# Context tokens of a feed-forward product: seven units in plain FP32 ahead, nine inside the seven-product steps, with the modulation and the second product's loads re-placed

## The chip, the cores and the metric

One Trainium2 chip; the kernel runs on 1 of its cores, as one launch. The metric is the device time of that launch in microseconds (us). Engines are called PE (matrix multiply), DVE (vector), ACT (scalar), POOL (GpSimd) and SP (the queue from which most DMAs are issued); each takes its own instructions in order and waits for others through semaphores. SBUF is the on-chip memory with 128 partitions, PSUM the eight accumulator banks that PE writes.

## The reference, cut to what matters

Two layers of one trunk run over 256 context tokens (two tiles of 128) and 1024 latent tokens (eight tiles). All is float32. Each layer ends in a feed-forward part for both streams; the second layer needs no context output.

```python
def _ffn_sublayer(x, shift, scale, gate, p):
    h = _modulate(_rms_norm(x, p['g_pre_ffn']), shift, scale)
    f = jnp.square(jax.nn.relu(h @ p['w_ff1'])) @ p['w_ff2']
    return x + gate * _rms_norm(f, p['g_post_ffn'])

    mod = s_lat @ w_mod[i] + b_mod[i]        # six shift/scale/gate vectors, latent stream
    mod_c = s_ctx @ w_mod[i] + b_mod[i]      # the same for the context stream
```

`w_ff1` is 1024 x 4096, `w_ff2` 4096 x 1024, `w_mod` 1024 x 6144 for each layer. Ahead of the feed-forward part each layer has a mixer (attention, short convolution, a state-space scan); the change leaves it alone.

## The kernel before, in words

**Split products.** A float32 operand is kept as two tiles in the reduced format fp32r: a high part (ACT, a cast) and a low part (source minus high part, DVE or POOL). `mm3` (lines 90 to 92) makes a product of three matmuls: high x high, high x low, low x high.

**First product, latent tokens.** For one of 16 units `j` of `w_ff1` the eight latent tiles are multiplied by Strassen's scheme in Winograd's form: seven products of halves in place of eight. `parts` makes the seven token operands `s0`..`s6` (512 tokens wide, from the four pairs of tiles that `all_pairs` normalises and transposes), `w1_parts` makes the seven weight operands of a unit from two raw loads `fraw`. `step1` runs the products on PE, seven times four times `mm3` = 84 matmuls of 512 columns, combines them with DVE (`u`, `c`), ACT (ReLU, then square) and POOL (`q`), and `combine` writes seven combinations to DRAM (`a7`) through ACT's DMA queue. PE's order in this whole part is the order in which the program is written; the other engines' instructions are placed by the scheduler of the language.

**First product, context tokens.** In the first layer this runs ahead of the 16 steps. `context` loops over all 16 units: `cut` splits each quarter of the weights (`craw` into `cwh`, `cwl`), `mm3` multiplies with the context tokens `hch`, `hcl`, 48 matmuls of 256 columns a unit; ReLU and square follow on ACT into two tiles `cab` with one buffer each, the combinations on POOL, seven small DMAs on ACT's queue. Between its blocks `side` weaves in `all_pairs`.

**Modulation of the next layer.** `mod_half` makes a quarter of one of the six vectors: four loads `mraw` of 256 KB through a ring of two buffers, and for each of 8 row blocks and each stream one DVE instruction (first L80, then L160) on an accumulator `acc`; at the end PE sums over partitions (L166, or L192 for gates). There are 24 such tasks, 8 of them for two streams. A list `bg` feeds them through `tick`: ten in steps 1 to 10, the others in the second product.

**Second product.** `second` goes over granules of the reduced dimension (one pair of units, then three times two pairs), with seven products each (`ORDER2`), five token pairs in the first layer, four in the second: 1470 and 1176 matmuls of 512 columns. It reads `a7` back (`ar`, ring of two) and the raw `w_ff2` (`graw`, in `w2`, four quarters of a unit at the start of a granule), splits both (`w2h`, `w2l`, `a2h`, `a2l`) and accumulates in SBUF. The last pair of units goes through `plain`.

Of the kernel before, what the change touches and what calls it, by code (L numbers as in the profile page):

```python
# [6 lines left out]
F32 = mybir.dt.float32  # L7
# [33 lines left out]
def emit(tc, A, depth=DEPTH):  # L41
# [127 lines left out]
    def mod_half(mp, L, v, half, streams, mb, nk, nb, off=False):  # L169
        accs = {s: mp.tile([P, mb], F32, tag="acc", name="acc", bufs=2 * 512 // mb) for s in streams}  # L170
# [16 lines left out]
        for s in streams:  # L187
# [5 lines left out]
            rows, rowb = (mp.tile([P, nk, mb], F32, tag="raw", name=n_, bufs=nb)[:, 0, :] for n_ in ("mrow", "mrowb"))  # L193
# [124 lines left out]
    class Strassen:  # L318

        def __init__(self, L, pairs, ctx=None):
# [7 lines left out]
        def load(self, p_, t, nb):  # L330
            xt = self.x[t] = p_.tile([P, D], F32, tag="x", name="x", bufs=nb)
            dma(xt, x1_d[t])
            normed(fp, xt, xt)
# [37 lines left out]
        def parts(self, p, what, alt="v"):  # L371
# [9 lines left out]
            for w in what:  # L381
                if w == "e":
# [6 lines left out]
                    put(5, s2, alt)  # L389
                    yield  # L390
                elif w == "a":
# [4 lines left out]
                    put(1, a12, "p")  # L396
# [3 lines left out]
                elif w == "b":  # L400
                    put(6, a21, alt)
                    yield
                else:
# [3 lines left out]
                    put(3, a22, "p")  # L407
# [9 lines left out]
        def w1_parts(self, j, out):  # L417
# [16 lines left out]
            tt("v", b22, b22, t1, ALU.subtract)  # L434
            t2 = b22
            put(5, t2, "v")
            put(4, t1, "v")
            put(1, b21, "p")
            put(6, t3, "v")
            yield  # L440
# [3 lines left out]
        def step1(self, j, w):  # L444
            st, n = self.st, self.n

            def t_(nm):
                return st.tile([P, n], F32, tag=nm, name=nm, bufs=1)
# [7 lines left out]

            A_, B_, C_ = psum("s"), psum("s"), psum("s")
            p1, p5, u2, q, c12, c21, c22, r11 = (t_(nm) for nm in ("p1", "p5", "u2", "q", "c12", "c21", "c22", "r11"))
# [8 lines left out]
            self.relu2(r11, A_[:, :n])  # L467
            prod(B_, 6, False, True)
            tt("v", c22, B_[:, :n], q, ALU.add)
            prod(C_, 2, False, True)  # L470
            tt("v", c12, C_[:, :n], u2, ALU.add)
            prod(B_, 3, False, True)
            tt("v", c21, B_[:, :n], p1, ALU.add)
            self.relu2(c22, c22)
            self.relu2(c12, c12)
            self.relu2(c21, c21)
            self.combine(j, (0, n), r11, c12, c21, c22, q, u2, p5)
# [5 lines left out]
        def combine(self, j, cs, r11, c12, c21, c22, q, u2, p5, e="v"):  # L483
# [7 lines left out]
            tt(e, q, c21, c22, ALU.add)  # L491
            tt(e, u2, q, r11, ALU.subtract)
            tt(e, c21, r11, c21, ALU.subtract)
            tt(e, p5, c12, u2, ALU.subtract)
# [3 lines left out]
        def context(self, side):  # L498

            hh, hl_ = self.hc  # L500
            halves = [(j, q) for j in range(16) for q in range(2)]
            ready = []

            def fetch():
                if halves:
                    j, q = halves.pop(0)
                    r = (wr if j % 2 == 0 else self.rw).tile([P, WU // 2], F32, tag="raw", name="craw", bufs=2)
                    dma(r, A["wu"][self.L, U_FF1 + j, :, q * 1024:(q + 1) * 1024])
                    raws.extend([r[:, 0:512], r[:, 512:1024]])

            def cut():
                if not raws:
                    fetch()
                if raws:
                    w = [self.cw.tile([P, 512], F32R, tag="cw" + x_, name="cw" + x_, bufs=6) for x_ in "hl"]
                    split(*w, raws.pop(0), "a", "v")
                    ready.append(w)

            raws = []
            for _ in range(5):  # L520
                cut()
            for j in range(16):
                ps = psum("s"), psum("s")
                for kh in range(2):
                    for c in range(2):
                        w = ready.pop(0)
                        for k in range(4):
                            o = slice(k * P, (k + 1) * P)
                            mm3(ps[c][:, :256], (w[0][:, o], w[1][:, o]), (hh[:, 4 * kh + k, :], hl_[:, 4 * kh + k, :]),
                                kh == 0 and k == 0, kh == 1 and k == 3)  # L530
                        cut()
                        side(j)
                ca, cb = (self.co.tile([P, 256], F32, tag=f"c{i}", name="cab", bufs=1) for i in range(2))
# [3 lines left out]
                self.combine(j, (self.n, self.n2), ca[:, :P], cb[:, :P], ca[:, P:], cb[:, P:], q, u2, p5, "p")  # L537
# [16 lines left out]
        def w2(self, gs):  # L554

            r = {}
            for q in (0, 2, 3, 1):
                for g in gs:
                    p_, nb = (wr, 2) if q == 0 else (self.rw, 6)
                    x = r[q, g] = p_.tile([P, WU // 2], F32, tag="raw", name="graw", bufs=nb)  # L560
# [1302 lines left out]
```

## Time and profile before

| | us |
|---|---|
| median of 3 runs | 3105.79 (3103.48 to 3110.14) |
| the profiled execution's own time | 3108.29 |
| its span, first to last instruction | 3106.5 |
| first layer, context part, 816.0 to 975.0 | 159.0 |
| first layer, 16 steps, 975.0 to 1304.5 | 329.5 |
| first layer, second product up to `plain`, 1304.5 to 1692.5 | 388.0 |
| first layer, `plain`, 1692.5 to 1764.0 | 71.5 |
| second layer, second product up to `plain`, 2767.5 to 3052.0 | 284.5 |

Over the span PE is busy 91%, DVE 72%, ACT 46%, POOL 41%; PE's mean granted clock is 0.944 of full speed. A row of a group reads: line, engine, operation, output <- inputs, shapes, count | busy time, mean ns of one | idle time of the engine just before, and what ended it. The mean is the duration of one instruction, and matmuls overlap, so their pace is read from the distance of two starts in the timeline, not from the mean. A float32 matmul of unsplit operands appears as two records.

### The profile page before, as it was taken

How to read it: one execution, taken by the hardware profiler on the slowest of the kernel's cores; microseconds unless marked ns; L12 is line 12 of the kernel's file. 1: busy time of each engine (PE TensorE's matmuls, PEld its weight loads, DVE VectorE, ACT ScalarE, POOL GpSimd, SP SyncE). 2: the span in 40 equal slices, each digit the busy share in tenths (PEclk: the TensorE clock that was granted, in tenths of full speed). 3: DMA queues.
4: the chain of work that ended last, by engine and by line, in shares of the span. 5: the costliest groups of instructions: out<-in, count | busy, mean ns of one | idle time of the engine just before them, and what ended most of it. 6: DMA issues, size and time to landing. Idle time of an engine off the chain costs nothing.

```text
span 3106.5 us, 41599 instructions
## 1 busy us (share of the span) xinstructions
PE 2818.2 (91%) x14606; PEld 2353.0 (76%) x14606; DVE 2237.0 (72%) x3323; ACT 1416.0 (46%) x2701; POOL 1284.3 (41%) x1151
## 2 busy tenths in 40 slices
PE   7988979999878999898997989999888699989998
PEld 5877878867766788787775778788766488868887
DVE  6688748776676896487897767348776866646888
ACT  3443447734454545452232454247634555545332
POOL 4465726676364222232225444326655422223233
PEclk9988999989988999999998899999889799999999
DMA  6245551253455554455543433441243244454443
GB/s 230 83 136 176 179 145 26 63 158 121 152 181 161 180 192 162 163 196 181 181 155 98 157 105 115 150 148 24 86 133 114 92 153 152 150 182 151 155 136 125
DMA packets 256849, 438.48 MB, mean 141 GB/s; under 512 B 23392, under 2 KB 132720, under 8 KB 256640
## 3 DMA queue, kind: packets, MB, share of 16 engines
q1 hardware_dynamic: 197536, 348.35, 34.9%
q10 hardware_dynamic: 52704, 75.92, 6.8%
q0 software_dynamic: 6400, 11.56, 1.5%
q8 instruction: 115, 1.88, 0.2%
q14 instruction: 94, 0.77, 0.1%
HBM read 310.79 MB, written 124.95 MB: 140 GB/s over the span
## 4 chain that ended last, share of the span: by engine, by line
PE 59%; DVE 17%; DMA 8%; issue 7%; POOL 5%; ACT 3%; SPq 0%; ACTq 0%; POOLq 0%; DVEq 0%
PE ps_s L90 16%; PE ps_s L91 15%; PE ps_s L92 15%; DMA mraw<-w_mod 3%; DVE acc L160 2%; PE ps_t L1235 2%; DVE yo L76 2%; PE ps_o L90 2%; PE ps_o L92 2%; PE ps_o L91 1%; DVE acc L76 1%; DVE w2l L76 1%; PE ps_g L1255 1%; PE ps_g L1256 1%; DVE graw L76 1%
## 5 line engine op out<-in xcount | busy, mean ns | idle before, releaser
L90 PE MATMUL ps_s<-w2h,a2h 128*128 128x512 f32 x1026 | 409.6, 400 | 35.3 <-DVE yo L76 13.6
L91 PE MATMUL ps_s<-w2l,a2h 128*128 128x512 f32 x1026 | 407.0, 397 | 0.5 <-DVE w2l L76 0.5
L92 PE MATMUL ps_s<-w2h,a2l 128*128 128x512 f32 x1026 | 405.4, 395 | 2.2 <-DVE a2l L76 2.2
L76 POOL TENSOR_TENSOR a2l<-ar,a2h 128x1280 fp32r<-128x1280 f32 (+1 forms) x56 | 165.5, 2956 | 404.4 <-ACT a2h L71 399.0
L71 ACT CAST a2h<-ar 128x1024 fp32r<-128x1024 f32 (+1 forms) x105 | 121.4, 1156 | 395.5 <-PE ps_s L91 238.5
L90 PEld LDWEIGHTS ps_s<-w2h,a2h 128*128 128x128 f32 x1026 | 196.9, 192 | 84.9 <-ACT a2h L71 11.9
L71 ACT CAST wh<-fraw 128x512 fp32r<-128x512 f32 x224 | 138.1, 621 | 235.2 <-PE ps_s L91 112.0
L76 POOL TENSOR_TENSOR wl<-fraw,wh 128x512 fp32r<-128x512 f32 x64 | 94.0, 1470 | 349.8 <-ACT wh L71 304.3
L160 DVE SCALAR_TENSOR_TENSOR acc<-mraw,svec,acc 128x256 f32<-128x256 f32 (+1 forms) x280 | 213.8, 777 | 34.0 <-DMA mraw<-w_mod 31.7
L92 PEld LDWEIGHTS ps_s<-w2h,a2l 128*128 128x128 f32 x1026 | 196.2, 191 | 45.4 <-DVE a2l L76 3.3
L91 PEld LDWEIGHTS ps_s<-w2l,a2h 128*128 128x128 f32 x1026 | 196.5, 192 | 41.0 <-DVE w2l L76 1.0
L76 DVE TENSOR_TENSOR w2l<-graw,w2h 128x1024 fp32r<-128x1024 f32 x102 | 165.5, 1624 | 23.9 <-ACT w2h L71 21.1
L1207 DVE TENSOR_REDUCE sm<-ps_s 128x1 f32<-128x512 f32 (+1 forms) x200 | 117.5, 592 | 35.0 <-PE ps_s L92 31.5
L76 DVE TENSOR_TENSOR wl<-fraw,wh 128x512 fp32r<-128x512 f32 x160 | 110.5, 692 | 29.6 <-ACT wh L71 27.4
L1220 ACT ACTIVATE P<-ps_s,sm 128x512 f32<-128x512 f32 (+1 forms) x200 | 120.0, 612 | 13.6 <-DVE sm L80 10.7
L76 DVE TENSOR_TENSOR fraw<-fraw 128x512 f32<-128x512 f32 x128 | 106.8, 836 | 23.6 <-POOL wl L76 19.3
L76 DVE TENSOR_TENSOR pl<-ps_t,ph 128x512 fp32r<-128x512 f32 x164 | 110.0, 684 | 12.6 <-ACT ph L71 11.8
L71 ACT CAST ph<-ps_t 128x512 fp32r<-128x512 f32 x164 | 94.8, 588 | 50.5 <-PE ps_t L1235 45.4
L71 ACT CAST w2h<-graw 128x1024 fp32r<-128x1024 f32 x106 | 110.6, 1044 | 6.9 <-PE ps_s L92 4.9
L76 DVE TENSOR_TENSOR yo<-ps_s,yo 128x512 f32<-128x512 f32 x144 | 94.7, 680 | 19.3 <-PE ps_s L92 19.3
L90 PE MATMUL ps_s<-hch,cwh 128*128 128x256 f32 x256 | 80.3, 313 | 29.0 <-ACT cab L480 27.7
L277 POOL TENSOR_TENSOR ss<-ss,expn 128x1 f32<-128x1 f32 x74 | 48.7, 658 | 134.0 <-DVE ss L276 130.4
(519 smaller groups left out, 9043.3 us busy)
## 6 DMA issues: line engine op xcount, KB each, us to landing
ar<-a SPq DMA_DIRECT2D x52, 640.0 KB
fraw<-wu SPq DMA_DIRECT2D x64, 512.0 KB
graw<-wu SPq DMA_DIRECT2D x64, 512.0 KB
ar<-a SPq DMA_DIRECT2D x53, 512.0 KB
wraw<-wu SPq DMA_DIRECT2D x48, 512.0 KB
mraw<-w_mod SPq DMA_DIRECT2D x96, 256.0 KB
a<-c ACTq DMA_DIRECT2D x92, 256.0 KB
x<-x SPq DMA_DIRECT2D x40, 512.0 KB
```

What stands on the lines that cost most here:

```text
L71: nc.scalar.copy(out=out, in_=in_)
L76: (nc.vector if e == "v" else nc.gpsimd).tensor_tensor(out=out, in0=a, in1=b, op=op)
L90: nc.tensor.matmul(out, lhsT=sh, rhs=mh, start=first, stop=False, skip_group_check=more)
L91: nc.tensor.matmul(out, lhsT=sh, rhs=ml, start=False, stop=False, skip_group_check=more)
L92: return nc.tensor.matmul(out, lhsT=sl, rhs=mh, start=False, stop=last, skip_group_check=more)
L160: nc.vector.scalar_tensor_tensor(out=acc, in0=raw, scalar=svec[:, k, s:s + 1], in1=acc, op0=ALU.mult, op1=ALU.add)
L277: nc.gpsimd.tensor_tensor(out=out, in0=out, in1=expn[:, :n], op=ALU.pow)
L1207: nc.vector.tensor_reduce(out=self.sm[i][:, b:b + 1], in_=self.sp_[i, b][:, :self.blocks[b][1]], axis=AX.X, op=ALU.max)
L1220: nc.scalar.activation(out=self.Pt[i][:, b0:b0 + bn], in_=self.sp_[i, b][:, :bn], func=AF.Exp, scale=SCALE, bias=self.sm[i][:, 5:6], accum ...
L1235: nc.tensor.transpose(ps[:, (2 * kk + i) * P:(2 * kk + i + 1) * P], self.Pt[i][:, kt * P:(kt + 1) * P], ident)
L1255: nc.tensor.matmul(self.av[:, :256], lhsT=vt_, rhs=ph[:, kk, :], start=kt == 0, stop=False)
L1256: nc.tensor.matmul(self.av[:, :256], lhsT=vt_, rhs=pl[:, kk, :], start=False, stop=kt == self.nkt - 1)
```

## The change

**Units 0 to 6 of the context part** (`ALONE = 7`) stay ahead of the steps and are multiplied unsplit: one float32 matmul of raw weights `craw` and unsplit tokens `hc32` in place of each `mm3`. `cut` and its splits go. The combinations move from POOL to DVE. `side` takes three items a call, in 28 calls in place of 64; all low parts of the pairs' operands go to DVE, half of the transposes' evictions and the normalising multiplication to ACT, and four token tiles are loaded at once.

**Units 7 to 15** go into the steps: `merged(j)`. Three of the four weight quarters that the context tokens need are operands of the step already (0, 1, 2); the fourth, `b12`, is split as an eighth (7). `cprod` adds 4 x 12 matmuls of 256 columns between the step's products, into one further PSUM bank; the context columns then ride with the latent ones through square, `combine` (640 columns in place of 512) and one DMA.

**In all steps of both layers** the order of products is 0, 4, 5, 1, 6, 2, 3 (before 0, 5, 4, 1, 6, 2, 3), and the weights are split in that order. The weights' slots are 6 in the first layer (before 9) and 8 in the second (before 11).

**All 24 modulation tasks** run in the steps: one at each step's end, and from step 7 on (and in step 4) a second one in its middle. The single-stream tasks come first; from step 7 on a step has one of one stream and one of two. A task's PE part now comes two tasks later.

**Second product.** The quarters of `w_ff2` are loaded by `quarter`, between the `ar` loads and in the order in which the products use them, and the queue keeps that order. The buffers for `ar` come first in their region. In the first granule all low parts are made by DVE. The gate load `G` keeps its place in the program's order too.

PE, first layer, the start of the context part (`x` token tiles, `cst` the identity for transposes). Before:

```order
L294 MATMUL ps_g<-cst,x 128x128 x2
L294 MATMUL ps_t<-cst,x 128x128 x2
L90 MATMUL ps_s<-hch,cwh 128x256
L91 MATMUL ps_s<-hcl,cwh 128x256
L92 MATMUL ps_s<-hch,cwl 128x256
```

Now:

```order
L1522 MATMUL ps_t<-cst,x 128x128 x4
L558 MATMUL ps_s<-hc_8327,craw 128x256 x16
L364 MATMUL ps_t<-cst,x 128x128 x2
L364 MATMUL ps_g<-cst,x 128x128 x2
L364 MATMUL ps_t<-cst,x 128x128 x2
L558 MATMUL ps_s<-hc_8327,craw 128x256 x4
```

One row stands where three stood, and the latent pairs' transposes (L364) come after the first unit's 16 matmuls.

PE, first layer, step 7, from the first product to the next. Before:

```order
L90 MATMUL ps_s<-s0h,wh 128x512
L91 MATMUL ps_s<-s0l,wh 128x512
L92 MATMUL ps_s<-s0h,wl 128x512
L90 MATMUL ps_s<-s5h,wh 128x512
L91 MATMUL ps_s<-s5l,wh 128x512
L92 MATMUL ps_s<-s5h,wl 128x512
```

Now:

```order
L90 MATMUL ps_s<-s0h,wh 128x512
L91 MATMUL ps_s<-s0l,wh 128x512
L92 MATMUL ps_s<-s0h,wl 128x512
L90 MATMUL ps_t<-hch,wh 128x256
L91 MATMUL ps_t<-hcl,wh 128x256
L92 MATMUL ps_t<-hch,wl 128x256
```

Behind a product of the latent tokens come the context tokens' matmuls with the same weights, into the bank `ps_t`.

SP, first layer, the loads of the second product (`a_0_i_g` is combination `i` of pair of units `g`). Before:

```order
L104 DMA graw<-wu 128x1024 x2
L104 DMA G<-g_0_1_88 128x1024
L104 DMA ar<-a_0_0_0_6748 128x2x640
L104 DMA ar<-a_0_1_0_6756 128x2x640
L104 DMA ar<-a_0_2_0_6764 128x2x640
L104 DMA graw<-wu 128x1024 x3
L104 DMA ar<-a_0_4_0_6780 128x2x640
```

Now:

```order
L104 DMA ar<-a_0_0_0_6748 128x2x640
L104 DMA graw<-wu 128x1024
L104 DMA ar<-a_0_1_0_6756 128x2x640
L104 DMA graw<-wu 128x1024
L104 DMA ar<-a_0_2_0_6764 128x2x640
L104 DMA graw<-wu 128x1024
L104 DMA ar<-a_0_4_0_6780 128x2x640
```

`G` no longer stands ahead of the first `ar`, and each quarter of the weights stands behind the `ar` of its own product.

```diff
     def mod_half(mp, L, v, half, streams, mb, nk, nb, off=False):
-        accs = {s: mp.tile([P, mb], F32, tag="acc", name="acc", bufs=2 * 512 // mb) for s in streams}
+        accs = {s: mp.tile([P, mb], F32, tag="acc", name="acc", bufs=6 if mb < 512 else 2) for s in streams}
...
         def w1_parts(self, j, out):
...
             put(0, b11, "v")
             tt("v", b11, b12, b11, ALU.subtract)
-            t1 = b11
-            put(2, b22, "p")
+            t1 = t2 = b11
+            put(4, t1, "v")
             yield
+            tt("v", t2, b22, t1, ALU.subtract)
+            put(5, t2, "v")
+            put(1, b21, "p")
+            if self.merged(j):
+                put(7, b12, "p")
             tt("v", b12, b22, b12, ALU.subtract)
             t3 = b12
...
             put(6, t3, "v")
+            put(2, b22, "p")
             yield
...
+        def merged(self, j):
+            return self.ctx is not None and j >= self.ALONE
+
-        def step1(self, j, w):
+        def step1(self, j, w, mid):
...
+            def cprod(i, c, kh):
+                if mg:
+                    hh, hl_ = self.hc
+                    for k in range(4):
+                        o = slice(k * P, (k + 1) * P)
+                        mm3(X_[:, c * 256:c * 256 + 256], (w[i][0][:, o], w[i][1][:, o]), (hh[:, 4 * kh + k, :], hl_[:, 4 * kh + k, :]),
+                            kh == 0 and k == 0, kh == 1 and k == 3, True)
...
             prod(A_, 0, True, True)
-            copy("a", p1, A_[:, :n])
+            copy("a", p1[:, :n], A_[:, :n])
+            cprod(0, 0, 0)
+            prod(C_, 4, True, True)
+            copy("a", p5[:, :n], C_[:, :n])
+            tt("p", q[:, :n], p1[:, :n], p5[:, :n], ALU.add)
             prod(B_, 5, True, True)
-            tt("v", u2, B_[:, :n], p1, ALU.add)
-            prod(C_, 4, True, True)
-            copy("a", p5, C_[:, :n])
-            tt("p", q, p1, p5, ALU.add)
+            tt("v", u2[:, :n], B_[:, :n], p1[:, :n], ALU.add)
             prod(A_, 1, False, True)
...
         def context(self, side):
...
-            for j in range(16):
+            for j in range(self.ALONE):
                 ps = psum("s"), psum("s")
                 for kh in range(2):
+                    r = raws.pop(0)
                     for c in range(2):
-                        w = ready.pop(0)
                         for k in range(4):
-                            o = slice(k * P, (k + 1) * P)
-                            mm3(ps[c][:, :256], (w[0][:, o], w[1][:, o]), (hh[:, 4 * kh + k, :], hl_[:, 4 * kh + k, :]),
-                                kh == 0 and k == 0, kh == 1 and k == 3)
-                        cut()
+                            o = slice(c * 512 + k * P, c * 512 + (k + 1) * P)
+                            nc.tensor.matmul(ps[c][:, :256], lhsT=r[:, o], rhs=self.hc32[:, 4 * kh + k, :], start=kh == 0 and k == 0,
+                                             stop=kh == 1 and k == 3)
                         side(j)
+                    fetch()
...
+                    if first and i in (0, 1, 2, 4):
+                        self.quarter(r, {0: 0, 1: 2, 2: 3, 4: 1}[i])
+                    elif i == 1:
+                        self.quarter(r, 1)
+                    for q in {5: (2,), 3: (0, 3)}.get(i, ()):
+                        self.quarter(r + 1, q)
...
-            for v in (1, 0, 2, 4, 3, 5):
-                for half in range(4):
-                    ss_ = (1, 0) if v < 2 or L + 1 < depth - 1 else (0,)
-                    bg.append(lambda v=v, half=half, ss_=ss_: mod_half(box["mp"], L + 1, v, half, ss_, 256, 2, 2))
+            tasks = [[(v, h) for v in vs for h in range(4)] for vs in ((2, 4, 3, 5), (1, 0))]
+            while tasks[0]:
+                if len(tasks[0]) <= 8 and tasks[1]:
+                    bg.append(lambda v=tasks[1][0][0], h=tasks[1].pop(0)[1]: mod_half(box["mp"], L + 1, v, h, (1, 0), 256, 2, 2))
+                bg.append(lambda v=tasks[0][0][0], h=tasks[0].pop(0)[1]: mod_half(box["mp"], L + 1, v, h, (0,), 256, 2, 2))
...
-            fs.step1(j, w)
-            if not last and 0 < j < 11:
-                tick(defer=True)
+            fs.step1(j, w, lambda: tick(defer=2) if j == 4 or j > 6 else None)
+            tick(defer=2)
             w = nxt
...
+        fs.ar = le.enter_context(pool("ar"))
+        la3 = le.enter_context(pool("a3"))
         lac = le.enter_context(pool("ac"))
         acc = {i: [lac.tile([P, 512], F32, name=f"acc{i}_{p}") for p in range(np_)] for i in (0, 5, 6)}
-        la3 = le.enter_context(pool("a3"))
-        fs.ar = le.enter_context(pool("ar"))
         fs.rw = le.enter_context(pool("rw2"))
-        if not last:
-            box["mp"] = le.enter_context(pool("mp2"))
```

More of the change, by code (lines that the diff above doesn't have):

```diff
@@ L192, in mod_half @@
             nc.tensor.matmul(ps[0:32, :mb], lhsT=ones[:, 0:32], rhs=accs[s], start=True, stop=True)
-            rows, rowb = (mp.tile([P, nk, mb], F32, tag="raw", name=n_, bufs=nb)[:, 0, :] for n_ in ("mrow", "mrowb"))
+            rows, rowb = (mp.tile([P, mb], F32, tag="row", name=n_, bufs=2) if mb < 512 else
+                          mp.tile([P, nk, mb], F32, tag="raw", name=n_, bufs=nb)[:, 0, :] for n_ in ("mrow", "mrowb"))
             b0, p0 = R_BG1 + w * D + h0, R_GPOST + w * D + h0
@@ L369, in part2, with parts @@
                 pass
-        def parts(self, p, what, alt="v"):
+        def parts(self, p, what, alt="p"):
             h = self.h32[p]
@@ L472, in step1 @@
+            cprod(2, 1, 1)
+            side(c22, 3)
+            side(c12, 2)
             prod(B_, 3, False, True)
[L473 to L477, printed above, removed]
+            tt("v", c21[:, :n], B_[:, :n], p1[:, :n], ALU.add)
+            end(c22)
+            end(c12)
+            end(c21)
+            r11, c12, c21, c22, q, u2, p5 = (x[:, :m] for x in (r11, c12, c21, c22, q, u2, p5))
@@ L498, in context @@
         def context(self, side):
-            hh, hl_ = self.hc
-            halves = [(j, q) for j in range(16) for q in range(2)]
-            ready = []
+            halves = [(j, q) for j in range(self.ALONE) for q in range(2)]
+            raws = []
             def fetch():
@@ L1485, in context_h @@
         def context_h(xns):
-            yield from prep_k(xc, xns, modc[L][1][1], *fs.hc, "tg", "vq")
+            mc = modc[L][1][1]
+            for k in range(KT):
+                ps = psum("tg"[k % 2])
+                for i, xn in enumerate(xns):
+                    nc.tensor.transpose(ps[:, i * P:(i + 1) * P], xn[:, k * P:(k + 1) * P], ident)
+                nc.vector.tensor_scalar(out=fs.hc32[:, k, :], in0=ps[:, :2 * P], scalar1=mc[:, 0, k:k + 1], scalar2=mc[:, 1, k:k + 1],
+                                        op0=ALU.mult, op1=ALU.add)
+                split(fs.hc[0][:, k, :], fs.hc[1][:, k, :], fs.hc32[:, k, :], "a", "v")
+                yield
         def end_tile(y, t, G):
@@ L1574, in emit @@
             fs.xq, fs.nh = he7.enter_context(pool("xq")), 2
[L1575 to L1576 removed]
+            for t in fs.mine[0] + fs.mine[1]:
+                fs.load(fs.xq, t, 4, True)
             def all_pairs():
                 for p in range(4):
[L1580 removed]
+                    for _ in fs.part1(p):
                         yield
[L1582 to L1586 removed]
+                    for t in fs.mine[p + 2] if p < 2 else ():
+                        fs.load(fs.xq, t, 4, True)
+                    yield from fs.parts(p, "eabc", "v")
                 he7.close()
[L1588 removed]
+                fs.slots(hae.enter_context(pool("w7b", "right")), 6)
             todo = all_pairs()
@@ L1594, in side @@
                 calls[0] += 1
-                if j >= 2 and not w70:
-                    for _ in range(2):
+                if calls[0] > 3 and not w70:
+                    for _ in range(3):
                         next(todo, None)
-                if calls[0] == 55:
+                if calls[0] == 27:
                     for _ in todo:
@@ L1653, in emit @@
         open_psum(s=7, g=1)
-        def tick2(x, gs):
-            if gs[-1] > 0 and x % 3 != 2:
-                tick(defer=True)
-        fs.second(yo, acc, tick2)
-        tick(len(bg) + 1)
-        rs = fs.w2([7])
+        pin[0] = True
+        fs.second(acc)
+        fs.quarter(4, 1)
+        pin[0] = False
+        rs = fs.rs
         ws = {}
```

125 lines of the change are left out of this document (59 added, 66 removed).

## The prediction

> **What bounds the kernel now.** I read the busy time by stage first, then in each stage what PE, the busiest engine, waits for. The table by windows has, for a stretch, the busy us of each engine (x instructions), PE's granted clock, the DMA share and GB/s; its rows are the context part, the 16 steps, the second product and `plain` of the first layer, and the second layer's second product:
>
> ```profile
> core 0: us, PE busy (x) PEld busy (x) DVE busy (x) ACT busy (x) POOL busy (x), PEclk, DMA share, GB/s
> 816.00:975.00 159.00, 115.08 (x834) 110.16 (x833) 111.59 (x151) 81.11 (x178) 85.58 (x93) 0.88 0.58 187
> 975.00:1304.50 329.50, 320.93 (x1411) 261.29 (x1412) 248.10 (x428) 160.51 (x269) 76.02 (x58) 0.99 0.50 165
> 1304.50:1692.50 388.00, 355.06 (x1516) 286.63 (x1516) 309.91 (x355) 133.42 (x141) 112.21 (x50) 0.95 0.53 174
> 1692.50:1764.00 71.50, 62.22 (x277) 49.95 (x276) 55.68 (x74) 22.81 (x46) 37.40 (x33) 0.93 0.33 117
> 2767.50:3052.00 284.50, 272.68 (x1178) 223.74 (x1178) 217.75 (x199) 119.82 (x135) 90.92 (x43) 0.98 0.48 157
> ```
>
> PE fills the steps (97%) and the second layer's product (96%). The gaps are in the context part (44 us idle, clock 0.88) and in the first layer's second product (33 us). The waits of PE, as total, count and longest, for the context part:
>
> ```profile
> PE ps_s L90 <- ACT cab L480: 33.5, 11, 7.6
> ```
>
> and for the second product of the first layer:
>
> ```profile
> PE ps_s L90 <- DVE yo L76: 12.7, 5, 8.5
> PE ps_g L192 <- DVE acc L160: 10.1, 1, 10.1
> PE ps_s L90 <- ACT a2h L71: 7.9, 1, 7.9
> PE ps_g L166 <- DVE acc L160: 7.0, 1, 7.0
> ```
>
> The first is the chain behind the context product: its PSUM banks come free only when ACT writes the single-buffered `cab`. Two of the others, 17.1 us, are modulation ends in PE's order.
>
> **Prices on PE.** Two matmuls of each split form, then a run of unsplit ones, from PE's timeline (start, time to the last end):
>
> ```profile
> 819.11 0.28 PE L91 MATMUL ps_s<-hcl,cwh 128*128 128x256 f32 x1
> 819.23 0.28 PE L92 MATMUL ps_s<-hch,cwl 128*128 128x256 f32 x1
> ...
> 1302.08 0.39 PE L92 MATMUL ps_s<-s3h,wl 128*128 128x512 f32 x1
> 1302.31 0.39 PE L90 MATMUL ps_s<-s3h,wh 128*128 128x512 f32 x1
> ...
> 18.01 2.31 PE L220 MATMUL ps_s<-sraw,svx 128*32 128x512 f32 x5
> ...
> 836.96 0.38 PE L358 MATMUL ps_t<-cst,x 128*128 128x128 f32 x2
> ```
>
> Starts are 0.12 us apart at 256 columns and 0.23 (0.229 over a step) at 512; a duration has 0.16 of latency above that (0.39 - 0.23). So an unsplit record of 512 columns costs (2.31 - 0.16) / 5 = 0.43, a matmul is two records, and at 256 columns half: 0.43 a matmul. A transpose costs (0.38 - 0.16) / 2 = 0.11. An unsplit matmul of 256 columns is not in the trace; it can cost from 0.36, what the three split ones cost, to 0.48 = 4 x 0.12. I take 0.43.
>
> The Trainium skill speaks against the change here: FP8 and Floating Point Precision, section "TensorE Precision Notes", has a full FP32 matmul take four passes through the array, where the split one takes three. The trace nearly agrees (0.86 / 0.23 = 3.7 passes at 512 columns). By four passes the 112 matmuls cost 53.8 us instead of 48.2, 6 us more than my sum.
>
> **Context part, 159 -> 76.** PE: 7 x 16 x 0.43 = 48.2, and 64 transposes, 7.0: 55. What ACT and DVE do instead, by these groups of the same stretch:
>
> ```profile
> L71 ACT CAST cwh<-craw 128x512 fp32r<-128x512 f32 x60 | 35.5, 615 | 15.6 <-POOL cq L76 5.7 <-DMA a<-cab 4.8 <-PE ps_s L91 2.6
> L481 ACT ACTIVATE cab<-cab 128x256 f32<-128x256 f32 x30 | 12.3, 416 | 0.4
> L480 ACT ACTIVATE cab<-ps_s 128x256 f32<-128x256 f32 x30 | 11.4, 379 | 38.8 <-DMA a<-cab 15.4 <-POOL cp L76 8.7 <-DMA a<-cq 7.5
> L282 ACT ACTIVATE junk<-x 128x1024 bf16<-128x1024 f32 x8 | 8.4, 1052 | 10.3 <-POOL cp L76 6.3 <-DMA x<-x 4.1
> ...
> L364 DVE TENSOR_SCALAR h<-ps_t,mod 128x256 f32<-128x256 f32 x16 | 8.6, 536 | 3.9 <-PE ps_t L358 3.9
> ```
>
> The 60-odd splits of `craw` go. ACT keeps 8 sums of squares (8.4), takes 8 scalings of the same size, which the trace lacks (8 x 1.05, by that row), half the evictions (16 x 0.4), 28 casts of tokens at 0.615 (17.2), 14 + 14 ReLU and square (11.1) and 7 casts for the first step (4.3): 56. DVE gets the low parts and combinations but loses the `cwl`, about 55 too. So three engines run level at 55. On top: about 4 us until the first `x` tiles, whose loads
>
> ```profile
> 823.33 1.27 SPq L104 DMA_DIRECT2D x<-x  x2
> ```
> ```profile
> 834.09 0.27 PE L358 MATMUL ps_t<-cst,x 128*128 128x128 f32 x1
> ```
>
> stand in SP's queue behind a store that waits for the mixer's last tokens (the first transpose now comes 11 us later, and PE would get to it at 816 + 6.9); 12 for waits on evictions and half clock, about a third of the old ones; and 5 to the first step:
>
> ```profile
> 975.00 0.80 PE L90 MATMUL ps_s<-s0h,wh 128*128 128x512 f32 x1 [5.78 <-ACT cab L480]
> ```
>
> which stays, since `fraw` of step 0 and the last `craw` use the same region. 55 + 4 + 12 + 5 = 76: -83. Bounds: 62 (no wait but the 7 of the ends), and 106 (55 at clock 0.88, and all 44 of idle time).
>
> **Steps, 329.5 -> 396.** A step takes 20.8 now: 84 x 0.229 = 19.2, and the end of a modulation task, where PE waits for DVE:
>
> ```profile
> 1062.97 0.61 PE L166 MATMUL ps_g<-cst,acc 128*128 128x1 f32 x4 [0.51 <-DVE mod L76]
> 1063.44 0.48 PE L90 MATMUL ps_s<-s0h,wh 128*128 128x512 f32 x1
> ```
>
> Steps 0 to 6 have one task of one stream, ended two tasks late: 19.9 each, and 4 for the start, 143. Merged steps add 48 x 0.12 = 5.8 on PE, so 25.1, plus 2.2 to 3.4 for the ends of three streams, in two places: 28.5. Steps 7 and 15, at the ends of the task list, lack some of that: 26.5. So 143 + 2 x 26.5 + 7 x 28.5 = 396: +66. What could be slower than PE is DVE; its groups in eight steps, 1041 to 1207:
>
> ```profile
> L160 DVE SCALAR_TENSOR_TENSOR acc<-mraw,svec,acc 128x256 f32<-128x256 f32 x91 | 54.1, 622 | 0.1
> L76 DVE TENSOR_TENSOR wl<-fraw,wh 128x512 fp32r<-128x512 f32 x40 | 27.2, 680 | 4.1 <-ACT wh L71 4.1
> L76 DVE TENSOR_TENSOR fraw<-fraw 128x512 f32<-128x512 f32 x32 | 21.9, 685 | 0.7
> ```
>
> By start distances such a 512-wide operation costs 0.60, a modulation one 0.40; the means are higher as DVE and POOL hold each other up:
>
> ```profile
> 1070.99 1.91 DVE L160 SCALAR_TENSOR_TENSOR acc<-mraw,svec,acc 128x256 f32<-128x256 f32 x2
> ```
> ```profile
> 1070.17 2.06 POOL L76 TENSOR_TENSOR wl<-fraw,wh 128x512 fp32r<-128x512 f32 x1 [5.31 <-ACT wh L71]
> ```
>
> (two take 1.91 where 0.8 would do, under a POOL split of 2.06). A merged step has 13 at 0.60, 4 of 640 columns at 0.75, 24 modulation operations at 0.40, some small ones, and four POOL operations that hold it by 0.9 each: 7.8 + 3 + 9.6 + 1.7 + 3.6 = 25.7, still under PE's 28.5. Bounds: 385 (no waits beyond the ends, 27 a merged step) and 436 (DVE at 0.62 for each modulation operation and 1.5 a hold, 33 to 34 a step).
>
> The Trainium skill has a rule for this: SBUF — State Buffer, section "Who interferes with whom", makes the pair of ports that DVE and GpSimd share an exclusive lock for the whole of an instruction. The 1.91 agrees. By it each POOL operation costs DVE up to its own length, some 0.7 us more than my hold; with four in a step that would bring DVE to 28.5, level with PE.
>
> **Second product, 388 -> 342, and `plain`, 71.5 -> 63.** The modulation leaves it, so both `acc` waits (17.1) go. The wait for `a2h` (7.9) came from the queue,
>
> ```profile
> 1304.35 0.33 SPq L104 DMA_DIRECT2D G<-g  x1
> 1304.73 11.04 SPq L104 DMA_DIRECT2D ar<-a  x3
> ```
>
> where `G` stands ahead of the first `ar` and the raw weights behind; it now reads in the order of use. DVE loses 14 tasks with their waits for loads:
>
> ```profile
> DVE acc L160 <- DMA mraw<-w_mod: 25.8, 16, 4.8
> ```
>
> 1470 x 0.229 = 337, and 5 for what is left at the start: 342, -46. Bounds: 337, and 370 if only the modulation's share goes. In `plain` the longest `yo` wait (8.5) goes: 63, -8.5; bounds 61 and 71.5.
>
> **Second layer, 284.5 -> 274.5.** Its waits are at the start:
>
> ```profile
> PE ps_s L90 <- ACT w2h L71: 7.4, 1, 7.4
> PE ps_s L90 <- ACT a2h L71: 3.0, 1, 3.0
> ```
>
> 1176 x 0.229 = 269, and 5 of these 10 stay: -10. Bounds 270 and 284.5. In its steps only the order of products and fewer weight slots change: nothing, since 84 matmuls of PE cover what DVE has without modulation (17 x 0.60 and little more, by the prices above); each us lost there a step would be 16.
>
> **Sum.** -83 + 66 - 46 - 8.5 - 10 = -81. The profiled execution took 3108.3 (span 3106.5 and 1.8 around it), 2.5 above the median, so 3027 for it and 3025 for a median. All lower bounds give 2991, all upper ones 3143.
>
> **Rivals.** *DVE sets the merged steps.* The sum above leaves it 3 us a step; if each POOL operation holds DVE for 1.5 us and each modulation operation keeps its mean of 0.62, a step is 33 in place of 28.1 (the mean of the nine): 9 x 4.9 = +44, 3069. For it: DVE is busy 248 of 329 us now, and half of its work in a step with a task is modulation. Against: nothing in these steps waits for DVE but task ends.
>
> *The gaps shrink less.* In the context part the `cab` tiles still have one buffer, the combinations now queue on DVE behind 28 low parts, and the second product keeps half of its gaps: 20 + 15 more, 3060.
>
> *The modulation's loads set the pace: slower than before.* All eight loads of a merged step go through two buffers,
>
> ```profile
> 1065.89 12.23 SPq L174 DMA_DIRECT2D mraw<-w_mod  x4
> ```
>
> four in 12 us here, 3.1 each, when SP waits for DVE to free a buffer. PE's order has the tasks' ends written into it, so it stops with all that stands behind: products, then DVE's `u` and ACT's evictions. From 28.1 / 8 = 3.5 us a load this decides; by 37.1 (4.6 a load) the whole gain is gone (81 / 9 = 9 a step). At 5 us a load a step is 40: 9 x 11.9 = +107, 3132. For it: PE did wait 10.1 and 7.0 for `acc` in the second product, with loads up to 4.8 late. Against: in the steps DVE is late by 0.1 in all ahead of 91 modulation operations, and ends lie two tasks back.
>
> *The context work costs in the steps what it saves ahead*: with 106 ahead, 420 in the steps and the second product at 365 the rest gives about 3100, no change.
>
> **How the numbers follow.** Forecast 0.56 (3000 to 3050 its own range), DVE 0.18, gaps 0.12, loads 0.10, no change 0.04. What this kernel's timing can tell from no change is 0.2%, 6 us. Faster: 0.56 + 0.18 + 0.12 = 0.86; same 0.04; slower 0.10. The range runs from 3000 (some bounds at their low end, 0.06 below it) to 3085 (above both middle rivals, 0.14 beyond it).
>
> **What would show it.** In the changed kernel: the first matmul of step 0 at 892 and not before 878; a merged step's period of 28.5, with DVE idle over 2 us in it; the last step done near 1288; the second product after it in 342 with no `acc` wait on PE; the second layer's two waits at its start down to 5. The prediction is wrong if merged steps take over 33, the context part over 106, or the second layer's steps slow by 1 us each.

## The result

The changed kernel takes 3035.4 us (median of 4 runs, 3033.5 to 3037.3) against 3108.0 for the kernel before on the same chip: a ratio of 0.9765, 95% interval 0.9751 to 0.9780. It is 73 us faster; the forecast was 3025, with a range of 3000 to 3085, from a sum of -81. The span of the profiled execution went from 3106.5 to 3035.2.

### The profile page after: what moved, and what is told of

The parts are those of the page before. It is cut to its first block, busy times and chain, and to the rows that moved or that the text cites. A ratio compares the mean times of both kernels' runs of the same rounds, so it can differ in the third digit from the quotient of the medians.

```text
span 3035.2 us, 40970 instructions
## 1 busy us (share of the span) xinstructions
PE 2813.3 (93%) x14494; PEld 2342.5 (77%) x14494; DVE 2148.8 (71%) x3301; ACT 1397.6 (46%) x2666; POOL 1181.1 (39%) x1062
## 5 line engine op out<-in xcount | busy, mean ns | idle before, releaser
L92 PE MATMUL ps_s<-w2h,a2l 128*128 128x512 f32 x1026 | 401.4, 391 | 0.0
L76 POOL TENSOR_TENSOR a2l<-ar,a2h 128x1280 fp32r<-128x1280 f32 (+1 forms) x50 | 146.7, 2935 | 390.8 <-ACT a2h L71 338.6
L76 POOL TENSOR_TENSOR wl<-fraw,wh 128x512 fp32r<-128x512 f32 x73 | 100.5, 1378 | 429.1 <-ACT wh L71 406.9
L160 DVE SCALAR_TENSOR_TENSOR acc<-mraw,svec,acc 128x256 f32<-128x256 f32 (+1 forms) x280 | 199.0, 727 | 34.2 <-DMA mraw<-w_mod 32.1
L76 DVE TENSOR_TENSOR wl<-fraw,wh 128x512 fp32r<-128x512 f32 x160 | 114.4, 716 | 27.3 <-ACT wh L71 27.2
L76 DVE TENSOR_TENSOR a2l<-ar,a2h 128x1024 fp32r<-128x1024 f32 (+1 forms) x55 | 77.8, 1415 | 45.3 <-ACT a2h L71 45.2
```

Of the source, the lines that this page charges most:

```text
L76: (nc.vector if e == "v" else nc.gpsimd).tensor_tensor(out=out, in0=a, in1=b, op=op)
L92: return nc.tensor.matmul(out, lhsT=sl, rhs=mh, start=False, stop=last, skip_group_check=more)
L160: nc.vector.scalar_tensor_tensor(out=acc, in0=raw, scalar=svec[:, k, s:s + 1], in1=acc, op0=ALU.mult, op1=ALU.add)
```

## The profile after

The table by windows of the changed kernel, with the same five stretches as in the prediction (context part, 16 steps, second product, `plain`, and the second layer's second product):

```profile
core 0: us, PE busy (x) PEld busy (x) DVE busy (x) ACT busy (x) POOL busy (x), PEclk, DMA share, GB/s
810.70:877.20 66.50, 57.30 (x291) 48.62 (x289) 51.38 (x109) 50.99 (x103) 6.12 (x10) 0.97 0.64 212
877.20:1291.50 414.30, 390.96 (x1886) 320.81 (x1886) 318.04 (x575) 172.57 (x313) 84.84 (x67) 0.97 0.54 179
1291.50:1637.00 345.50, 338.10 (x1474) 277.85 (x1474) 249.48 (x227) 133.97 (x141) 97.20 (x42) 0.99 0.46 156
1637.00:1705.00 68.00, 60.03 (x267) 48.51 (x266) 48.31 (x66) 21.48 (x43) 29.94 (x29) 0.92 0.28 101
2703.00:2979.40 276.40, 270.64 (x1181) 222.50 (x1180) 215.64 (x201) 119.12 (x135) 85.05 (x39) 0.99 0.48 161
```

| part | before | after | difference | forecast |
|---|---|---|---|---|
| context part | 159.0 | 66.5 | -92.5 | -83 |
| 16 steps | 329.5 | 414.3 | +84.8 | +66 |
| second product, first layer | 388.0 | 345.5 | -42.5 | -46 |
| `plain` | 71.5 | 68.0 | -3.5 | -8.5 |
| second product, second layer | 284.5 | 276.4 | -8.1 | -10 |
| everything else | 1874.0 | 1864.5 | -9.5 | 0 |

Of the last row, 4.7 us are the second layer's first step, 24.9 us here and 29.6 before (23.9 to 25.6 in all runs below), which was not forecast. The rest of it is no effect that can be read from these runs: the first layer's mixer ended anywhere from 807.9 to 815.2 us in the executions shown in this document, at 809.2 here and at 814.5 in the kernel before. Differences of 5 us between two spans are therefore read by stage below.

In the context part PE no longer waits for `cab` between units, and PE's granted clock is 0.97, where it was 0.88. Its first unit shows the price of an unsplit matmul, which the trace of before did not have:

```profile
810.69 7.07 PE L558 MATMUL ps_s<-hc,craw 128*128 128x256 f32 x32
...
820.14 0.33 PE L364 MATMUL ps_t<-cst,x 128*128 128x128 f32 x1 [2.05 <-ACT x L337]
...
877.18 0.80 PE L90 MATMUL ps_s<-s0h,wh 128*128 128x512 f32 x1 [5.77 <-ACT cab L519]
```

Sixteen matmuls are 32 records in 7.07 us, so (7.07 - 0.16) / 16 = 0.43 each. The wait for the first `x` is 2.05 us, the one at the first step 5.77.

In the second product the two `acc` waits are gone. What is left at its start is the wait for the first weights, their high part `w2h` and then their low part `w2l`, and the same holds in the second layer (the waits of PE from 1290 to 1330, then from 2703 to 2735):

```profile
PE ps_s L90 <- ACT w2h L71: 3.8, 1, 3.8
PE ps_s L91 <- DVE w2l L76: 2.5, 1, 2.5
...
PE ps_s L90 <- ACT w2h L71: 4.0, 1, 4.0
PE ps_s L91 <- DVE w2l L76: 1.8, 1, 1.8
```

The steps are where the time is above the forecast. By the starts of their first matmuls, steps 0 to 6 take 23.3, 23.6, 19.9, 21.0, 21.1, 24.3 and 27.7 us (sum 160.9, forecast 143); the merged ones, the last up to its end at 1291.5, take 25.8, 27.8, 27.8, 27.4, 27.6, 27.2, 35.1, 28.4 and 26.3 (sum 253.4, forecast 252.5). The two worst stalls of PE, in steps 6 and 13:

```profile
1032.43 0.79 PE L90 MATMUL ps_s<-s3h,wh 128*128 128x512 f32 x1 [4.50 <-DVE c L76]
```
```profile
1221.34 0.50 PE L166 MATMUL ps_g<-cst,acc 128*128 128x1 f32 x4
1225.72 1.01 PE L166 MATMUL ps_g<-cst,acc 128*128 128x1 f32 x4 [3.88 <-DVE mod L76]
```

and some of DVE's instructions ahead of the two:

```profile
1024.90 1.70 DVE L80 TENSOR_SCALAR acc<-mraw,svec 128x256 f32<-128x256 f32 x2 [2.58 <-DMA mraw<-w_mod]
...
1031.70 0.68 DVE L76 TENSOR_TENSOR c<-ps_s,q 128x512 f32<-128x512 f32 x1
...
1215.63 1.47 DVE L80 TENSOR_SCALAR acc<-mraw,svec 128x256 f32<-128x256 f32 x1 [2.47 <-DMA mraw<-w_mod]
...
1220.93 1.01 DVE L160 SCALAR_TENSOR_TENSOR acc<-mraw,svec,acc 128x256 f32<-128x256 f32 x2 [1.31 <-DMA mraw<-w_mod]
...
1225.52 0.14 DVE L76 TENSOR_TENSOR mod<-ps_g,pk 128x2 f32<-128x2 f32 x1
```

DVE stands at a modulation operation whose load has not landed; the addition `c` (which frees a PSUM bank), or the `mod` that empties `ps_g` between the ends of two streams, is behind it in DVE's order, and PE waits for that.

## The experiments

Ratios are against the kernel before on the same chip, with 95% intervals; "the changed kernel" is 0.9765 [0.9751, 0.9780].

**A ring of three buffers for the modulation's loads**

```diff
-        accs = {... bufs=6 if mb < 512 else 2) ...}
+        accs = {... bufs=4 if mb < 512 else 2) ...}
...
-    mod_half(box["mp"], L + 1, v, h, (0,), 256, 2, 2)
+    mod_half(box["mp"], L + 1, v, h, (0,), 256, 2, 3)
```

> The changed kernel with three buffers in place of two for the modulation's loads mraw (and four accumulators in place of six, for the room). Theory: the 18 us that the steps cost above the forecast (414 for 396) come from modulation operations on DVE that wait for a load, with the additions behind them that free PE's banks: steps 5, 6 and 13, with 24, 28 and 35 us, fall to 21, 22 and 28, the whole to 3018 to 3024. Rival: DVE's order and amount of work does it, not the loads; then 3033 to 3037.

Measured: 3014.4 us, ratio 0.9693 [0.9673, 0.9713]. Steps 1, 6 and 13 went from 23.6, 27.7 and 35.1 to 20.7, 24.6 and 26.9; step 5 stayed at 24.3. The table by windows for steps 8 to 13, of the changed kernel, then of this run:

```profile
1063.90:1236.80 172.90, 163.52 (x863) 137.89 (x862) 145.92 (x279) 69.22 (x133) 34.80 (x26) 0.98 0.57 192
```
```profile
1061.20:1221.70 160.50, 158.99 (x862) 136.17 (x861) 137.99 (x268) 69.92 (x132) 35.30 (x25) 1.00 0.60 200
```

and DVE's two groups of modulation in these steps, again of the changed kernel and of this run:

```profile
L160 DVE SCALAR_TENSOR_TENSOR acc<-mraw,svec,acc 128x256 f32<-128x256 f32 x131 | 69.8, 562 | 17.9 <-DMA mraw<-w_mod 17.7
...
L80 DVE TENSOR_SCALAR acc<-mraw,svec 128x256 f32<-128x256 f32 x18 | 10.5, 584 | 2.5 <-DMA mraw<-w_mod 2.5
```
```profile
L160 DVE SCALAR_TENSOR_TENSOR acc<-mraw,svec,acc 128x256 f32<-128x256 f32 x120 | 61.0, 522 | 2.5 <-DMA mraw<-w_mod 1.3
...
L80 DVE TENSOR_SCALAR acc<-mraw,svec 128x256 f32<-128x256 f32 x18 | 10.8, 598 | 3.6 <-DMA mraw<-w_mod 3.6
```

DVE's idle time ahead of modulation falls from 20.4 to 6.1 us, and the six steps from 172.9 to 160.5, with PE busy in 99% of them. Up to the second product's first matmul the steps take 399.1 us, for 418.7 in the changed kernel. That is 19.6 us less, as much as the steps took above the forecast: it was the price of waiting for loads. (The run also has two accumulators fewer, for the room.) This version beats both kernels, by 21 us below the changed one.

**The same room in finer pieces**

```diff
-    mod_half(box["mp"], L + 1, v, h, (0,), 256, 2, 2)
+    mod_half(box["mp"], L + 1, v, h, (0,), 256, 1, 4)
```

> The changed kernel with the modulation's loads cut in two: four buffers of 128 KB in place of two of 256 KB, the same room. Theory: with four loads under way a buffer is asked for again sooner, DVE waits less for mraw, 3025 to 3032. Rival: what counts is the bytes in the ring, or SP's queue with twice the issues, then 3035 to 3045.

Measured: 3026.1, ratio 0.9728 [0.9708, 0.9749]. From the steps' first matmul to the second product's first the run took 410.3 us, for 418.7 in the changed kernel; step 13 was still at 33.4, after 35.1. The theory holds, with a gain less than half of a third buffer's.

**Finer pieces of a ring of three, and a ring of three without the second task of step 4**

```diff
-    mod_half(box["mp"], L + 1, v, h, (0,), 256, 2, 3)
+    mod_half(box["mp"], L + 1, v, h, (0,), 256, 1, 6)
```

> Ring of three in finer pieces: six buffers of 128 KB in place of three of 256 KB. Theory: what the ring of three leaves of DVE's waits for the first load of a task (14.5 us) and the stalls of steps 5 and 6 (3 us each) shrinks further, 3008 to 3012. Rival: the ring is long enough with three and SP's issues double, 3014 to 3020.

```diff
-    fs.step1(j, w, lambda: tick(defer=2) if j == 4 or j > 6 else None)
+    fs.step1(j, w, lambda: tick(defer=2) if j > 6 else None)
```

> Ring of three, without the second modulation task in step 4 (each later task one place later, the last one ends in step 15). Theory: steps 5 and 6 are at 24.5 because three tasks fall on them; they fall to 21 to 22, step 15 gains 1 to 2, the whole is 3009 to 3013. Rival: the work only moves to the later steps, which have no room on DVE, and the second product's first loads come later behind the last task's: 3014 to 3020.

Measured: 3018.2 (3008.5 to 3018.6), ratio 0.9709 [0.9681, 0.9737], and 3014.2, ratio 0.9706 [0.9681, 0.9732]. Neither is told apart from the plain ring of three, and both times lie where the rival had them, at 3014 to 3020. By stage both do what was expected in steps 5 and 6 (20.4 and 22.6; 20.9 and 22.6, from 24.3 and 24.6), 5 to 6 us in all (the first's steps are those of its execution of 3008.5 us); in the second, the second product's second matmul then starts 7.7 us after its first, in place of 3.0.

**All 16 context units ahead**

```diff
-        ALONE = 7
+        ALONE = 16
```

(with the pairs' preparation spread over the 64 calls)

> The changed kernel with all 16 context units ahead and unsplit, none in the steps. Theory: a further unit ahead costs 7.5 us (16 x 0.43 on PE and some waiting), nine of them +67; the steps lose 9 x 48 x 0.12 = 52 and little more; 3050. Rival: with a full pipeline of units the cab buffers stall PE again as before, 10 us a unit: 3075 or more.

Measured: 3091.9, ratio 0.9937 [0.9920, 0.9953]. The context part took 135.0 us, from 812.8 to 947.8: nine units more cost 68.5, 7.6 each, as the theory had it. No `cab` stall like that of before, which the rival needed, came back, by PE's waits:

```profile
PE ps_s L558 <- ACT cab L519: 4.8, 3, 2.2
```

But the steps did not lose the 52 us of context matmuls; up to the second product's first matmul they took 400.8 us for 418.7. The table for steps 8 to 13, for a row of 863 matmuls in the changed kernel above:

```profile
1132.60:1296.00 163.40, 138.26 (x574) 109.84 (x573) 134.97 (x281) 63.19 (x105) 24.54 (x20) 0.93 0.58 186
```

They take 27.2 us each with 288 matmuls less, so without the context matmuls PE is not what sets a step with two modulation tasks. Neither forecast of the time had this.

**A ring of three with all units ahead**

> Ring of three, with all 16 context units ahead (so no context matmuls in the steps). In the run with all units ahead steps 9 to 15 kept 25 to 28 us though PE had 5.7 us less to do, so that something else paces a step with two modulation tasks. Theory: the two-buffer ring does, eight loads of 3.4 us; with three buffers these steps fall to 22 to 24, and the whole to 3045 to 3055. Rival: DVE's own work does, 24 modulation operations and the additions, at 24 us busy; then they stay at 26 to 27 and the whole is near 3075.

Measured: 3080.6, ratio 0.9914 [0.9882, 0.9946]. The same steps, and what PE waits for in them:

```profile
1125.40:1285.80 160.40, 136.52 (x575) 109.99 (x574) 138.35 (x271) 62.14 (x104) 24.69 (x19) 0.90 0.57 184
```
```profile
PE ps_g L166 <- DVE mod L76: 21.3, 6, 4.9
```

26.7 us a step: the theory that the ring alone sets them falls, and the rival's 26 to 27 is met. DVE is busy 23.1 of them and waits 2.4 for loads; PE stands 3.5 us a step between the ends of two streams, until DVE comes to the `mod` that empties the bank.

**Less modulation work in these steps.** In the run before, the second stream's accumulation stops after its first row block; that part of the modulation is left out, so the second layer's vectors for that stream are not the true ones.

```diff
-                    else:
+                    elif not (mb < 512 and len(streams) == 2 and s == 0 and k0 + k > 0):
                         mod_acc(accs[s], raw[:, k, :], k0 + k, s)
```

> The run with a ring of three and all units ahead, with part of the modulation left out: in the eight tasks of two streams the second stream's accumulation stops after its first row block, so that a step with two tasks has 17 modulation operations on DVE in place of 24, with the same eight loads and the same ends on PE. Theory: DVE's work sets these steps at 27 us; 7 operations of 0.4 to 0.7 less bring them to 22 to 24. Rival: the loads or PE's ends set them; then they stay at 26 to 27.

Measured: 3057.9, ratio 0.9848 [0.9809, 0.9886].

```profile
1118.90:1264.80 145.90, 135.55 (x574) 109.13 (x574) 118.03 (x237) 62.73 (x105) 23.94 (x19) 0.93 0.64 208
```

DVE's modulation in the six steps, of the run before and of this one:

```profile
L160 DVE SCALAR_TENSOR_TENSOR acc<-mraw,svec,acc 128x256 f32<-128x256 f32 x122 | 70.1, 582 | 14.8 <-DMA mraw<-w_mod 14.1
```
```profile
L160 DVE SCALAR_TENSOR_TENSOR acc<-mraw,svec,acc 128x256 f32<-128x256 f32 x87 | 47.2, 542 | 9.2 <-DMA mraw<-w_mod 8.2
```

24.3 us a step in the mean (21.7 to 26.1), just above the 22 to 24 of the theory and 2.4 less than before, where DVE is busy 3.4 less (138.4 to 118.0 in six steps). The loads and the ends are the same, so DVE's work bears on these steps. Its waits for loads fell with it, from 14.6 to 8.2 us in the six steps, and how much of the 2.4 belongs to each was not told apart: what is shown is that DVE's queue, work and waits together, sets them.

So a two-task step costs 26.7 us with the context matmuls, where PE is busy throughout, and without them, where DVE's queue sets it. Nine units fit into time that DVE takes anyway and are cheap there: 18 us in place of 68 ahead, and with rings of three 4 us (399.1 for 395.0 up to the second product's first matmul) in place of 66.

**The seven units ahead in split form**

```diff
-                            nc.tensor.matmul(ps[c][:, :256], lhsT=r[:, o], rhs=self.hc32[...], ...)
+                            mm3(ps[c][:, :256], (w[0][:, o], w[1][:, o]), (hh[...], hl_[...]), ...)
+                        cut()
```

> The changed kernel with the seven units ahead multiplied in split form, as in the kernel before (casts of craw on ACT, low parts on DVE, four buffers). Theory: PE has 7 x 48 x 0.12 = 40 us in place of 48, but ACT gets 28 casts of 0.62 more, 17 us, and DVE as many low parts; with both at about 50 of 66 us now the part takes 78 to 82 in place of 66, in sum 3048. Rival: PE sets this part and the split form is the shorter one, 3027.

Measured: 3054.5, ratio 0.9822 [0.9804, 0.9841]. From the mixer's last product to the first step 84.7 us, for 68.0 in the changed kernel, with ACT and DVE busy 67 us each, for 51:

```profile
813.00:900.00 87.00, 60.75 (x420) 57.43 (x418) 67.41 (x137) 66.91 (x133) 9.33 (x13) 0.85 0.58 188
```

The form that is dearer on PE is the shorter one in the whole. What PE waits for in this stretch speaks for ACT, which writes both `cab` and `x` (in the changed kernel they are 5.8 and 2.1):

```profile
PE ps_s L90 <- ACT cab L519: 8.8, 2, 5.6
PE ps_t L364 <- ACT x L337: 7.5, 3, 3.7
```

That the casts and low parts on ACT and DVE are the cause is argued from this, and not shown apart: the run has four buffers for the split weights where the kernel before had six, and more of them were not tried.

**The second product's loads in the old order**

```diff
-                    if first and i in (0, 1, 2, 4):
-                        self.quarter(r, {0: 0, 1: 2, 2: 3, 4: 1}[i])
...
+                    if i == self.ORDER2[0]:
+                        for q in (0, 2, 3, 1):
+                            self.quarter(r, q)
```

> The changed kernel with the second product's loads in the old order: all four quarters of the weights at a granule's start, behind the first ar load. Theory: the waits at the start of both layers' second products come back, +8 in the first layer and +10 in the second, 3053. Rival: these loads were hidden anyway and the waits came from G or from the modulation, then 3035 to 3039.

Measured: 3056.0, ratio 0.9821 [0.9801, 0.9840], 0.0056 above the changed kernel, 17 us. From the first matmul of the second product to `plain` it is 6.8 us longer in the first layer (347.8 for 341.0), and 5.7 in the second (277.2 for 271.5). 12 to 19 us behind the start PE waits for `a2h` and `a2l`, 3.5 and 1.5 us in the first layer and 1.6 and 1.3 in the second, where the changed kernel has no wait. The rest of the difference lies in parts that have the same order. The order of loads is worth some 13 to 17 us, a little less than expected.

**The modulation put back**, first with the new task list, then with the old one, then with the old order of loads as well:

```diff
-            fs.step1(j, w, lambda: tick(defer=2) if j == 4 or j > 6 else None)
-            tick(defer=2)
+            fs.step1(j, w, lambda: None)
+            if 0 < j < 11:
+                tick(defer=2)
...
+        def tick2(x, gs):
+            if not last and gs[-1] > 0 and x % 3 != 2:
+                tick(defer=2)
+        fs.second(acc, tick2)
+        tick(len(bg) + 1)
```

> The changed kernel with the modulation put back: ten tasks in steps 1 to 10, fourteen in the second product, with the accumulators and row buffers of before. My theory (the prediction's): the two waits for acc in PE's order and DVE's waits for loads come back to the first layer's second product, +17 to +30 us on its 348; the steps lose the second task, about -30 on their 414. Net -13 to 0 against the changed kernel's 3035. Rival: moving the modulation is where the gain comes from; then the sum is 3050 or more.

> As the first run (modulation back in the second product), but with the task list of before too: the eight tasks of two streams come first, in steps 1 to 8, so that the second product gets 14 streams of modulation in place of 21. Theory after the first run: in the second product the modulation's loads wait in SP's queue for DVE to free a buffer, and the ordered loads of ar and graw, of which each is now asked for just before its product, wait behind them; PE then waits for a2h. With 14 of 21 streams two thirds of that loss is left: the second product 405, the steps 388, in sum about 3065. Rival: what costs is only DVE's work on the streams; then the second product is 365 and the sum 3030.

> Both undone: modulation as before and the second product's loads in the old order; what is left is the context tokens' part. Theory (the two interact): with all weights of a granule asked for ahead, a modulation load that waits holds up less; the second product takes about 380 as in the kernel before, the second layer's 284, the steps 388: about 3050. Rival (the parts add up): the run before plus the 21 us of the load order, 3085.

Measured: 3090.9 (0.9938 [0.9921, 0.9956]), 3077.7 (0.9889 [0.9867, 0.9911]) and 3073.0 (0.9875 [0.9859, 0.9892]). The first was expected at 3022 to 3035; that theory fell. The second came near its theory in the second product (405) and above it in the whole (3065); the third lies between its two forecasts, 3050 and 3085. From the second product's first matmul to `plain` the three take 442.8, 408.4 and 401.4 us, for 341.0 in the changed kernel, while up to there the steps save only 27 to 36. What SP's queue waits for, and PE, in the second product of the first of the three:

```profile
SPq L174 <- DVE acc L160: 121.6, 34, 13.8
```
```profile
PE ps_s L90 <- ACT a2h L71: 32.2, 4, 13.7
PE ps_g L166 <- DVE mod L76: 27.5, 9, 11.3
```

The modulation's loads (L174) stand in SP's queue for 121.6 us until DVE has freed a buffer, with the loads of the products' operands behind them; PE then waits for `a2h`. In the two other runs the queue's wait is 72.1 and 81.5 us and PE's for `a2h` 12.6 and 12.2; in the kernel before they are 66.7 and 7.9. The two are largest together in the first run, which points to the queue without proving it. PE's 27.5 us for `mod` end with DVE, and what held DVE there was not followed.

So the parts do not add up. With the modulation in the second product the new order of loads changes nothing that can be told (0.9889 against 0.9875, intervals overlap); with the modulation out of it, it gives 0.0056. And moving the modulation gives 0.0054 (0.9875 to 0.9821) with the old order and 0.0124 (0.9889 to 0.9765) with the new one. The context part alone, with both others undone, gives 0.0125 of the 0.0235, by the last run. It isn't a full undo: the second product there is 21 us slower than in the kernel before (401.4 for 380.0), with that kernel's task list and order; its buffers for raw weights, the queue's fixed order and the first granule's low parts on DVE stay the new ones. Which of these costs the 21 us was not tried.

## Why the prediction was right, and where it was not

**The sum.** Right in sign and nearly in size, -73 for -81: four of five terms lie within 10 us of what was measured, and the two larger errors, -9.5 in the context part and +18 in the steps, pull in opposite directions. Part of the closeness is luck. In the two traces the five stretches together changed by -61.8, and another -9.5 came from the rest of the kernel, to which the forecast gave nothing. Step 0 began at 877.2, ahead of the 878 named as its bound, only because the context part began 5.3 us earlier than before; its length is within the bound.

**Context part, 66.5 for 76.** The price of an unsplit matmul was right, 0.43. By the four passes that the Trainium skill (FP8 and Floating Point Precision, section "TensorE Precision Notes") states for full FP32, an estimate is 4 x 0.12 = 0.48; the measured 0.43 is 3.6 times the split matmul's 0.12, so the trace does not fully agree. The three level engines were right too, at 57, 51 and 51 us busy. Mis-sized was "12 for waits on evictions and half clock, about a third of the old ones", a term without a row of its own: PE was idle for 9.2 us in all, 5.8 of them at the first step (forecast 5) and 2.1 for `x` (forecast 4), and 1.3 were left for the 12. That the `cab` chain shrinks was right, and it went altogether; that was not for the smaller number of units, since with 16 of them it stays away. Whether the casts on ACT or the combinations on POOL fed it was not told apart.

**Steps, 414 for 396.** The step of the prediction that failed is "Steps 0 to 6 have one task of one stream, ended two tasks late: 19.9 each, and 4 for the start": they took 160.9 in place of 143. Their stalls are modulation operations that wait for loads with `u` and `c` behind them on DVE; with three buffers these seven steps take 153.9, and with the same room in six small ones 148.0. Step 4 also has a second task, which the sum left out: without it, in the ring of three, steps 5 and 6 fall from 24.3 and 24.6 to 20.9 and 22.6, and the seven take 146.5. A sign of this stood in the trace of before: there too PE waits for `u` and `c` in steps 0 and 1, 4.2 us in all, so "nothing in these steps waits for DVE but task ends" was not quite so. The merged steps came out at the forecast sum, 253.4 for 252.5, and that is luck: two errors cancel. PE's 25 us plus the ends do bound them once the loads are on time, but at 26.7 (PE is busy in 99%), so that the ends cost 1.7, and not the 3.4 that made 28.5; the stalls for loads, which the sum did not have, made up for it. At the same time DVE's queue needs as much, since without any context matmul these steps stay at 26.7. The room of 3 us that the prediction gave DVE was not there: its sum of DVE's prices, 25.7, is even above the 23 us that DVE is busy, but the waits for loads and the handing over of `ps_g` were left out of it.

**The rivals.** "DVE sets the merged steps" is borne out only where the context matmuls are gone, and at 27 and not 33 us a step; with them PE takes as long. A modulation operation has a mean of 0.52 to 0.56 us in these steps, and not 0.62, and holds by POOL of 1.5 us each do not fit into the 23 to 24 us that DVE is busy in a step. "The modulation's loads set the pace" was right in place and in chain, as shown in steps 6 and 13, and the third buffer prices it at 21 us, a fifth of the 107 it was given: steps 8 to 13 took 28.8 us, 3.6 for each of eight loads, just about the 3.5 from which it decides, and not 5. What the prediction had against it, DVE late by 0.1 us in all ahead of 91 operations, was true for the steps of before with one task; with two it was 20 us in six steps.

**Second product and `plain`.** -42.5 for -46 and -3.5 for -8.5. Both `acc` waits went, as said. `plain`'s `yo` wait stayed (7.7 for 8.5), so this term was wrong: PE still stands 8 us early in `plain`, and about as long in every run that has the modulation out of the second product. How much of the old `a2h` wait was due to `G` and how much to the weights was not told apart. What the prediction did not see is that moving the modulation and re-ordering the loads depend on each other, by the waits through SP's queue.

**Second layer.** -8.1 for -10: the waits at the start fell from 10.4 to 5.8 us, nearly as forecast. Its steps stayed at 19.3 us each, so fewer weight slots and the new order of products cost nothing; that the first of them takes 4.7 less was not foreseen, and why was not tried.

## What to carry to other kernels

Work for one engine is cheap where another engine already sets the pace: find a stage that is bound by DVE's queue and put matmuls there, rather than shorten the stage in which they are. When a queue issues loads in program order, a load that waits for a ring buffer holds up the loads behind it. Here just-in-time order paid only once the slow ring was out of that queue (0.0056 of the time, against nothing that could be told), so such edits have to be judged together. Count waits for loads as part of an engine's time when an in-order engine is said to have room: here one more buffer of 256 KB was worth 21 us beside the change's 73.

## What the runs showed of the hardware that was not expected

An unsplit float32 matmul of 256 columns costs 0.43 us, against 0.36 for the three reduced-format ones that replace it, and its version of the context part was still 17 us shorter over 112 matmuls. PE's granted clock was lower where PE had long gaps: 0.88 in the context part with 44 us of idle time, 0.97 with 9 (and 1.00 with 10 in the run with a ring of three). In step 13 the twelve matmuls of 512 columns behind a stall of 4 us started 0.43 us apart in place of 0.23, so that this stall cost 12 x 0.2 = 2.4 us beyond its own length. Two of the twelve in PE's timeline:

```profile
1228.02 0.63 PE L90 MATMUL ps_s<-s2h,wh 128*128 128x512 f32 x1
1228.45 0.63 PE L91 MATMUL ps_s<-s2l,wh 128*128 128x512 f32 x1
```
